# The two latent norms are emitted earlier in the projection stream of a hybrid FoX/MLA layer

## The chip, the cores and the metric

The kernel runs on one core of a Trainium2 chip. The metric is the device time of one execution in microseconds (us), the median of three runs. TensorE (PE, with its weight loads PEld), VectorE (DVE), ScalarE (ACT) and GpSimd (POOL) each work through one list of instructions in a fixed order. Loads are issued from SyncE's queue (SP), in order as well, and a few stores from POOL's.

## The reference, cut to what matters

One layer for 512 prompt tokens and 64 sample tokens, 576 together. One projection makes the FoX queries, keys and values and the two MLA latents, and each latent gets an RMS norm before it is used:

```
z = rmsnorm(x, g_attn) @ w_in
q, k, v, f_lin, q_c, c_kv, k_r = split(z)      # 512 | 512 | 512 | 8 | 384 | 256 | 32
fox  = softmax(q k' + forget) v                # 8 heads x 64
q_full = rmsnorm(q_c, g_q) @ w_q_up            # query latent, 384
c_kv   = rmsnorm(c_kv, g_kv)                   # key latent, 256, also an output
mla  = softmax(q_lat c_kv' + q_rope k_r') ...  # 8 heads
x = x + [fox, mla] @ w_out
x = x + (silu(conv(gate)) * conv(value)) @ w_down
```

## The kernel before, in words

Activations lie with features on the partitions and the 576 tokens along a row. A projection tile of 128 features (`in_tile`) is a product of 48 matmuls: 8 input chunks, 3 passes each (weights and activations are split in a high and a low part), for two halves of 288 tokens. The halves go to two PSUM banks that `psg` hands out. After the start these are the two banks with the tag `g`. DVE evacuates each half (L449, L455, L458 for keys, queries, values of a head pair, L542 for a latent), and only then may PE write that bank again.

FoX has four head pairs, p = 0 to 3. `fox_gemm(p)` projects the pair's keys, then its queries, then its values. An optional function `between` is called after the keys and before the queries. Behind pair 1 come the five latent tiles, a = 0 and 1 for the key latent (`craw`), a = 2 to 4 for the query latent (`qcr`). `sq_sum` squares the tiles of a latent and adds them up on DVE, POOL and ACT. `latent_norm` then does this: `col_sums` (L229) sums the squares over the partitions with a matmul against ones, one for each half, each shown as two passes in the trace, into two `g` banks; L261 evacuates them; L250 and L251 on ACT and L255 to L257 on DVE make the reciprocal root; L549 on DVE scales each tile of the latent.

Attention of a head is made of scores (L516, L517, L358, or for MLA L702 to L704), a softmax on DVE, ACT and POOL, transposes (L374) and values (L389). Each pair also has a sample part (L523, L524, L427, L437, for MLA L721, L722). `A` holds the stacked operands of a head, two buffers, filled by SP's L476 to L512, for MLA by L476 to L478 and L695 to L698, after the head before the last has given its buffer back. `mla_caches` loads the old rotary keys (`kr_T`, L633) into the buffer `spt` that the sample part of pair 3 gives back behind L437; L637, L638 and L639 split them into `cf`, which the last matmul of the MLA sample scores, L722, reads.

The emission order comes from a planner: five streams of work are interleaved by written costs and due times (`yield`). The build then sets the order of each engine from data, buffers and that emission order. So a moved call can shift much that stands behind it. `POOL` also issues the store of the key latent, `o_lat`.

Of the kernel before, what the change touches and what calls it, by code (L numbers as in the profile page):

```python
# [30 lines left out]
C_GA, C_GF, C_GL, C_GQ, C_GKV = 0, 8, 16, 24, 27  # L31
# [40 lines left out]
def build(nc, tc, io):  # L72
# [5 lines left out]
    V, S, G, PE = nc.vector, nc.scalar, nc.gpsimd, nc.tensor  # L78
# [9 lines left out]
    def raw():  # L88

        if ffn[0]:  # L90
            rawn[0] += 1
            tag, bufs = FRAW[rawn[0] % len(FRAW)]
            return sb([P, 580], F32, tag, bufs)
        return sb([P, 580], F32, "raw", RAW)
# [25 lines left out]
    def pick(kind):  # L120

        n = cyc[kind] = cyc.get(kind, -1) + 1
        return ENG[kind][n % len(ENG[kind])]
# [10 lines left out]
    def tt(kind, dst, a, b, op):  # L134
        (V if pick(kind) == "v" else G).tensor_tensor(dst, a, b, op=op)  # L135
# [76 lines left out]
    def evac(op, dst, ps, r=slice(0, P)):  # L212
        for hf, (o, w) in enumerate(HA):
            op(dst[:, o:o + w], ps[hf][r, :w], slice(o, o + w))

    def square(eng, t):
        s = raw()[:, :T]
        if eng is S:
            S.activation(s, t, AF.Square)
        else:  # L220
            eng.tensor_tensor(s, t, t, op=ALU.mult)
        return s

    def col_sums(tiles, w=ones):

        ps = psg()
        for hf, (o, wd) in enumerate(HA):
            for n, t in enumerate(tiles):
                PE.matmul(ps[hf][:, :wd], lhsT=w, rhs=t[:, o:o + wd], start=(n == 0), stop=(n == len(tiles) - 1))  # L229
        return ps  # L230

    def sq_sum(tiles, sq="sq", add="acc"):
        acc = None
        for t in tiles:
            s = square({"a": S, "v": V, "g": G}[pick(sq)], t)
            if acc is None:
                acc = s
            else:
                tt(add, acc, acc, s, ALU.add)
        return acc  # L240
# [18 lines left out]
    def rstd(ps, n, out):  # L259
        v, y, a = (raw()[:, :T] for _ in range(3))  # L260
        evac(lambda d, p, c: V.tensor_scalar(d, p, 1.0 / n, EPS, op0=ALU.mult, op1=ALU.add), v, ps)  # L261
        rstd_of(v, y, a, out)
# [28 lines left out]
    def in_tile(u, M=P):  # L291
        hl = wload(io["w_in"][u], 1024)
        ps = psg()
        gemm(ps, M, hl, xhl, HA)
        return ps
# [150 lines left out]
    def fox_gemm(p, between=None):  # L446
        ps = k0 if p == 0 else in_tile(p)
        k = raw()
        evac(lambda d, p, c: V.tensor_tensor(d, p, R[:, c], op=ALU.mult), k, ps)  # L449
        G.dma_start(io["o_k"][p], k[:, :T])  # L450
        if between:
            between()
        ps = in_tile(4 + p)
        q = raw()
        evac(lambda d, p, c: V.scalar_tensor_tensor(d, p, FOX_SCALE, R[:, c], op0=ALU.mult, op1=ALU.mult), q, ps)  # L455
        ps = in_tile(8 + p)
        v = raw()
        evac(lambda d, p, c: V.tensor_tensor(d, p, R[:, c], op=ALU.mult), v, ps)  # L458
        G.dma_start(io["o_v"][p], v[:, :T])
        return q, k, v  # L460
# [76 lines left out]
    craw, qcr = [], []  # L537
# [7 lines left out]
    def latent_norm(t, n, col, acc):  # L545
        r = raw()[:, :T]
        rstd(col_sums([acc]), n, r)
        for a in range(n // P):
            V.scalar_tensor_tensor(t[a], t[a], par[:, col + a:col + a + 1], r, op0=ALU.mult, op1=ALU.mult)  # L549
# [7 lines left out]
    fx = {0: fox_gemm(0)}  # L557
# [186 lines left out]
    def s_gemm():  # L744
        for p in range(1, 4):
            if p >= 2:
                yield ("after", ("stack", 2 * (p - 2) + 1), 0)
            fx[p] = fox_gemm(p, gates if p == 1 else None)
            yield ("done", 23.1, ("up", p))
            if p == 1:  # L750
                for a in range(5):
                    latent(a)
                    if a == 2:
                        rope_key()
                    if a == 1:
                        acc_c = sq_sum(craw)
                    if a == 4:
                        acc_q = sq_sum(qcr)
                    yield ("done", 7.7, ("lat", a))
            if p == 2:  # L760
                latent_norm(craw, 256, C_GKV, acc_c)
                latent_norm(qcr, 384, C_GQ, acc_q)
                for a in range(2):
                    G.dma_start(io["o_lat"][a], craw[a])
        mla_keys()
        yield ("done", 0, ("keys", 0))
        for p in range(4):
            if p == 0:
                yield ("after", ("stack", 5), 0)
            else:  # L770
                yield ("after", ("stack", 6 + 2 * p - 1), 0)
            if p % 2 == 0:
                q_rope(p // 2)
                yield ("done", 2.2, ("rope", p))
            mla_up(p)
            yield ("done", 5, ("up", 4 + p))
# [201 lines left out]
    for hf, (o, w) in enumerate(HC):  # L978
# [24 lines left out]
        v, y, a, r3 = (raw()[:, :w] for _ in range(4))  # L1003
# [121 lines left out]
```

## Time and profile before

| what | value |
| --- | --- |
| median of 3 runs | 796.04 us (795.74 to 796.42) |
| profiled execution | 796.07 us, span 794.2 us |
| PE busy | 766.0 us (96%) |
| PEld busy | 738.3 us (93%) |
| DVE, ACT, POOL busy | 504.4 us (64%), 340.9 us (43%), 265.5 us (33%) |
| granted TensorE clock | 0.995 of full speed |
| chain that ended last | PE 82%, DVE 5%, ACT 4%, DMA 4% |

The span runs from the first to the last instruction of the profiled execution. 1.9 us of that execution's time lie outside it. PE is busy nearly throughout, so what counts is where PE waits: any us in which PE does nothing is a us of the time.

### The profile page before, as it was taken

How to read it: one execution, taken by the hardware profiler on the slowest of the kernel's cores; microseconds unless marked ns; L12 is line 12 of the kernel's file. 1: busy time of each engine (PE TensorE's matmuls, PEld its weight loads, DVE VectorE, ACT ScalarE, POOL GpSimd, SP SyncE). 2: the span in 40 equal slices, each digit the busy share in tenths (PEclk: the TensorE clock that was granted, in tenths of full speed). 3: DMA queues.
4: the chain of work that ended last, by engine and by line, in shares of the span. 5: the costliest groups of instructions: out<-in, count | busy, mean ns of one | idle time of the engine just before them, and what ended most of it. 6: DMA issues, size and time to landing. Idle time of an engine off the chain costs nothing.

```text
span 794.2 us, 14259 instructions
## 1 busy us (share of the span) xinstructions
PE 766.0 (96%) x5582; PEld 738.3 (93%) x5582; DVE 504.4 (64%) x940; ACT 340.9 (43%) x612; POOL 265.5 (33%) x392
## 2 busy tenths in 40 slices
PE   8899999998999999999999999999999999999994
PEld 7899899887878889999999999999999999999994
DVE  6966735978676764656866424776326667675455
ACT  7426622568567773223434223333213443433232
POOL 5234532444132320432432221443122343332135
PEclk9999999999999999999999999999999999999997
DMA  9475325264545631222222232222222222222313
GB/s 328 142 205 143 99 80 156 93 180 134 146 105 127 156 106 36 75 89 86 75 83 77 65 106 89 80 81 62 80 100 89 96 81 80 80 67 85 95 53 119
DMA packets 33811, 83.97 MB, mean 106 GB/s; under 512 B 6007, under 2 KB 9351, under 8 KB 33745
## 3 DMA queue, kind: packets, MB, share of 16 engines
q1 hardware_dynamic: 31520, 78.55, 33.1%
q0 software_dynamic: 1008, 3.19, 1.1%
q10 hardware_dynamic: 1216, 1.33, 0.5%
q8 instruction: 44, 0.72, 0.4%
q14 instruction: 23, 0.18, 0.1%
HBM read 64.12 MB, written 5.49 MB: 88 GB/s over the span
## 4 chain that ended last, share of the span: by engine, by line
PE 82%; DVE 5%; ACT 4%; DMA 4%; issue 2%; SPq 1%; POOL 1%; POOLq 0%; ACTq 0%; DVEq 0%
PE g L209 36%; PE s L209 19%; PE t L209 12%; PE g L437 3%; PE g L990 1%; DMA mix<-xT 1%; PE t L374 1%; PE s L721 1%; ACT p L325 1%; DVE B L381 1%; PE s L990 1%; ACT wh L194 1%; PE s L890 1%; PE t L990 1%; DVE wh L135 1%
## 5 line engine op out<-in xcount | busy, mean ns | idle before, releaser
L209 PE MATMUL g<-xs,wh 128*128 128x288 f32 x1680 | 239.4, 296 | 0.4 <-ACT wh L194 0.2
L209 PEld LDWEIGHTS g<-xs,wh 128*128 128x128 f32 x1680 | 227.7, 188 | 1.8 <-ACT wh L194 0.4
L194 ACT ACTIVATE wh<-wr 128x1024 fp32r<-128x1024 f32 (+4 forms) x106 | 99.7, 943 | 195.1 <-PE g L209 75.4
L135 POOL TENSOR_TENSOR wh<-wr,wh 128x1024 fp32r<-128x1024 f32 (+3 forms) x51 | 111.3, 2182 | 161.2 <-ACT wh L194 131.1
L209 PE MATMUL s<-xs,wh 128*128 128x288 f32 (+1 forms) x504 | 75.3, 295 | 2.6 <-DVE xs L266 2.6
L209 PEld LDWEIGHTS s<-xs,wh 128*128 128x128 f32 (+1 forms) x504 | 69.0, 186 | 3.3 <-ACT wh L194 2.0
L135 DVE TENSOR_TENSOR wh<-wr,wh 128x1024 fp32r<-128x1024 f32 (+5 forms) x55 | 60.9, 1111 | 14.0 <-ACT wh L194 13.8
L209 PE MATMUL t<-xs,wh 128*128 128x288 f32 (+1 forms) x348 | 52.4, 295 | 1.4 <-DVE wh L135 1.4
L209 PEld LDWEIGHTS t<-xs,wh 128*128 128x128 f32 (+1 forms) x348 | 47.7, 185 | 1.8 <-DVE wh L135 1.6
L909 POOL COPY KR<-raw 128x2 f32<-128x2 f32 x33 | 15.6, 474 | 92.4 <-DVE raw L907 92.4
L331 POOL TENSOR_SCALAR p<-p,small 128x128 f32<-128x128 f32 (+2 forms) x48 | 27.3, 570 | 49.2 <-DVE small L326 37.3
L913 DVE SCALAR_TENSOR_TENSOR raw<-raw,par 128x578 f32<-128x578 f32 x22 | 33.4, 1518 | 15.4 <-ACT raw L912 15.4
L939 ACT ACTIVATE raw<-raw 128x578 f32<-128x578 f32 x22 | 15.1, 688 | 58.2 <-DVE raw L914 58.1
L325 ACT ACTIVATE p<-s,small 128x128 f32<-128x128 f32 (+1 forms) x64 | 33.6, 526 | 8.3 <-DVE small L360 6.5
L381 DVE TENSOR_TENSOR B<-t,B 128x512 fp32r<-128x512 f32 (+1 forms) x64 | 29.8, 480 | 6.5 <-ACT B L128 6.3
L128 ACT ACTIVATE B<-t 128x512 fp32r<-128x512 f32 (+1 forms) x64 | 26.3, 435 | 15.9 <-PE t L374 15.2
L360 DVE TENSOR_REDUCE small<-s 128x1 f32<-128x128 f32 (+1 forms) x64 | 30.6, 479 | 2.8 <-PE s L358 1.2
L913 DVE SCALAR_TENSOR_TENSOR raw<-pq,par,raw 128x578 f32<-128x578 f32 x11 | 24.0, 2181 | 11.1 <-ACT raw L912 11.1
L209 PE MATMUL g<-sk,wh 128*128 128x288 f32 x186 | 30.6, 297 | 0.4 <-ACT wh L194 0.4
L209 PE MATMUL s<-sk,wh 128*128 128x288 f32 x192 | 30.8, 296 | 0.2 <-ACT wh L194 0.2
L209 PE MATMUL s<-sv,wh 128*128 128x288 f32 x192 | 30.6, 295 | 0.0
L209 PE MATMUL g<-sv,wh 128*128 128x288 f32 x186 | 29.8, 296 | 0.0
(377 smaller groups left out, 1571.7 us busy)
## 6 DMA issues: line engine op xcount, KB each, us to landing
wr<-w_up SPq DMA_DIRECT2D x44, 512.0 KB
wr<-w_dn SPq DMA_DIRECT2D x24, 384.0 KB
wr<-w_in SPq DMA_DIRECT2D x16, 512.0 KB
A<-pq SPq DMA_DIRECT2D x32, 256.0 KB
mix<-xT SPq DMA_DIRECT2D x16, 288.0 KB
wr<-w_out SPq DMA_DIRECT2D x8, 512.0 KB
A<-pq SPq DMA_DIRECT2D x24, 128.0 KB
sk<-k_c SPq DMA_DIRECT2D x4, 512.0 KB
```

The costliest lines, as they stand in the source:

```text
L128: S.activation(dst, src, AF.Copy)
L135: (V if pick(kind) == "v" else G).tensor_tensor(dst, a, b, op=op)
L194: S.activation(hl[:, 0, a:b], r[:, a:b], AF.Copy)
L209: PE.matmul(ps[hf][:M, :w], lhsT=hl[:, wi, kc * M:(kc + 1) * M], rhs=acts[kc][:, xi, o:o + w], start=(kc == 0 and pi == 0), stop=(kc == n ...
L325: S.activation(p, src, AF.Exp, bias=nm, accum_out=sm[:, 0:1])
L331: (G if e == "g" else V).tensor_scalar(p, p, sm[:, 1:2], 1.0, op0=ALU.mult, op1=ALU.mult)
L360: V.reduce_max(nm[:, 0:1], s[:, :W], axis=AX.X, negate=True)
L381: V.tensor_tensor(ptj[:, 1, off:], t[:, :w], f(ptj[:, 0, off:]), op=ALU.subtract)
L437: PE.matmul(out, lhsT=v[:, j, :], rhs=spt[:, j, :], start=(j == 0), stop=(j == 8))
L909: G.tensor_copy(cs[:, ch, 0:2], u[:, 512:514])
L913: V.scalar_tensor_tensor(t, u[:, 1:579], par[:, C_CW + 44 + ch:C_CW + 44 + ch + 1], t, op0=ALU.mult, op1=ALU.add)
L990: PE.matmul(ps[:, :w], lhsT=whl[m][:, wi, kc * P:(kc + 1) * P], rhs=g2[kc][:, xi, c], start=(kc == 0 and pi == 0), stop=(kc == n - 1 and p ...
```

## The change

The norm of the key latent and the store of it are emitted right behind the last latent tile, before pair 2 is projected. The norm of the query latent is emitted inside the projection of pair 2, between its keys and its queries. Before, both stood behind the whole projection of pair 2. Nothing is computed differently.

```
@@ s_gemm
-            fx[p] = fox_gemm(p, gates if p == 1 else None)
+            fx[p] = fox_gemm(p, (None, gates, lambda: latent_norm(qcr, 384, C_GQ, acc_q), None)[p])
...
                     if a == 4:
                         acc_q = sq_sum(qcr)
+                    if a == 4:
+                        latent_norm(craw, 256, C_GKV, acc_c)
+                        for b in range(2):
+                            G.dma_start(io["o_lat"][b], craw[b])
                     yield ("done", 7.7, ("lat", a))
-            if p == 2:
-                latent_norm(craw, 256, C_GKV, acc_c)
-                latent_norm(qcr, 384, C_GQ, acc_q)
-                for a in range(2):
-                    G.dma_start(io["o_lat"][a], craw[a])
```

**PE at the last latent tiles.** The rows are matmuls with output, inputs, shape and count, in PE's order; L209 is the projection, L229 the column sums. A minus marks rows of before, a plus those of now.

```order
-L209 MATMUL g<-xs,wh 128x288 x240
-L229 MATMUL g<-raw,ones 128x288
+L209 MATMUL g<-xs,wh 128x288 x96
+L229 MATMUL g<-raw,ones 128x288 x2
+L209 MATMUL g<-xs,wh 128x288 x48
+L229 MATMUL g<-raw,ones 128x288 x2
+L209 MATMUL g<-xs,wh 128x288 x194
```

Two latent tiles, the keys, queries and values of pair 2 were one run of 240 matmuls, and the four column sums stood one by one among the attention work behind it. Now the two sums of the key latent stand behind the last latent tile and the two of the query latent behind the keys of pair 2. Then the rest of pair 2 and the first half of pair 3 follow without a break, while pair 3's 144 matmuls stood behind the attention work before.

**DVE at the same place, before.** From the last latent tile (L542) through the keys of pair 2 (L449).

```order
L542 TENSOR_TENSOR mix<-g,R 128x288 x2
L135 TENSOR_TENSOR raw<-raw 128x576
L449 TENSOR_TENSOR raw<-g,R 128x288 x2
L490 COPY sk<-raw 128x64
L135 TENSOR_TENSOR wh<-wr,wh 128x1024
```

**DVE at the same place, now.**

```order
L542 TENSOR_TENSOR mix<-g,R 128x288 x2
L261 TENSOR_SCALAR raw<-g 128x288 x2
L135 TENSOR_TENSOR raw<-raw 128x576
L255 TENSOR_TENSOR raw<-raw 128x576
L256 SCALAR_TENSOR_TENSOR raw<-raw 128x576
L257 SCALAR_TENSOR_TENSOR raw<-raw 128x576
L449 TENSOR_TENSOR raw<-g,R 128x288
L549 SCALAR_TENSOR_TENSOR mix<-mix,par,raw 128x576 x2
L449 TENSOR_TENSOR raw<-g,R 128x288
L261 TENSOR_SCALAR raw<-g 128x288
L490 COPY sk<-raw 128x64
```

The norm of the key latent now stands around the two evacuations of pair 2's keys: four instructions ahead of the first L449 (the L135 in between, which adds the last squares of the query latent, was there before), and the two L549 between the first and the second.

**PE behind the last FoX sample part, before.** L209 is here the query up-projection, L669 the key and value up-projection of an MLA pair, L374 and L389 belong to FoX head 7.

```order
L209 MATMUL g<-xs,wh 128x288 x15
L374 MATMUL t<-ident,p_2413 128x128
L374 MATMUL t<-ident,p_2424 128x128
L374 MATMUL t<-ident,p_2435 128x128
L209 MATMUL g<-xs,wh 128x288
L389 MATMUL o<-B,v 128x512
L669 MATMUL g<-xs,wh 128x512 x6
L374 MATMUL t<-ident,p_2424 128x128
L374 MATMUL t<-ident,p_2435 128x128
L389 MATMUL o<-B,v 128x512
L722 MATMUL s<-cf,sl 128x384
```

**PE at the same place, now.**

```order
L209 MATMUL g<-xs,wh 128x288 x11
L374 MATMUL t<-ident,p_2413 128x128
L374 MATMUL t<-ident,p_2424 128x128
L374 MATMUL t<-ident,p_2435 128x128
L722 MATMUL s<-cf,sl 128x384
L389 MATMUL o<-B,v 128x512
L669 MATMUL g<-xs,wh 128x512 x12
```

L722, which reads `cf`, moved ahead of the first L389, six L669 and two L374.

**SP at the same place, before.** Loads from the stack of the second MLA head (the second L476) to `kr_T`.

```order
L476 DMA A<-pq 64x512
L695 DMA A<-KR 2x512
L696 DMA A<-KR 4x512
L478 DMA A<-pq 64x2x512 x2
L698 DMA A<-qr 32x512
L477 DMA A<-pq 64x1024 x2
L698 DMA A<-qr 32x512 x2
L185 DMA wr<-w_qu 128x384
L686 DMA sl<-qr 32x64 x2
L626 DMA sv<-c_tok 128x1024
L633 DMA spt<-kr_T 32x1024
```

**SP at the same place, now.**

```order
L476 DMA A<-pq 64x512
L478 DMA A<-pq 64x2x512 x2
L695 DMA A<-KR 2x512
L477 DMA A<-pq 64x1024 x2
L696 DMA A<-KR 4x512
L698 DMA A<-qr 32x512 x3
L185 DMA wr<-w_qu 128x384
L626 DMA sv<-c_tok 128x1024
L633 DMA spt<-kr_T 32x1024
```

The two small loads L686 moved ahead of this piece; the rest is the same set.

## Rows read from the trace of the kernel before

**Rows 1.** Windows: length, then busy us (count) of PE, PEld, DVE, ACT, POOL; clock, DMA.

```profile
116.00:134.70 18.70, 18.70 (x143) 18.70 (x142) 9.33 (x11) 4.61 (x7) 7.07 (x5) 1.00 0.39 108
134.70:146.00 11.30, 10.59 (x62) 7.82 (x60) 10.58 (x27) 7.23 (x18) 2.69 (x6) 1.00 0.65 173
165.40:190.00 24.60, 22.52 (x149) 18.32 (x148) 21.55 (x53) 17.79 (x48) 14.17 (x19) 1.00 0.56 159
```

**Rows 2.** Timeline of PE: start, length, instruction, shapes, count, idle time ahead and releaser.

```profile
134.71 0.65 PE L229 MATMUL g<-raw,ones 128*128 128x288 f32 x2
135.19 0.38 PE L340 MATMUL t<-ident,raw 128*128 128x128 f32 x2
...
144.08 0.30 PE L374 MATMUL t<-ident,p 128*128 128x128 f32 x1 [0.28 <-DVE B L381]
...
145.42 0.45 PE L516 MATMUL s<-A 128*128 128x384 f32 x1 [0.43 <-ACT p L325]
```

**Rows 3.** Timeline of DVE, 108 to 147 us.

```profile
115.83 0.46 DVE L542 TENSOR_TENSOR mix<-g,R 128x288 f32<-128x288 f32 x1 [2.74 <-PE g L209]
117.60 2.96 DVE L135 TENSOR_TENSOR raw<-raw 128x576 f32<-128x576 f32 x1 [1.32 <-POOL raw L221]
...
122.19 0.46 DVE L449 TENSOR_TENSOR raw<-g,R 128x288 f32<-128x288 f32 x1 [1.26 <-PE g L209]
...
134.91 0.46 DVE L458 TENSOR_TENSOR raw<-g,R 128x288 f32<-128x288 f32 x1 [1.83 <-PE g L209]
135.40 0.46 DVE L261 TENSOR_SCALAR raw<-g 128x288 f32<-128x288 f32 x1
...
140.26 0.76 DVE L255 TENSOR_TENSOR raw<-raw 128x576 f32<-128x576 f32 x1 [0.28 <-ACT raw L251]
...
146.32 1.53 DVE L549 SCALAR_TENSOR_TENSOR mix<-mix,par,raw 128x576 f32<-128x576 f32 x2
```

**Rows 4.** Timeline of POOL, the subtraction that splits a projection tile's weights.

```profile
117.53 2.42 POOL L135 TENSOR_TENSOR wh<-wr,wh 128x1024 fp32r<-128x1024 f32 x1
```

**Rows 5.** Timeline of PE, 165 to 230 us.

```profile
191.46 0.23 PE L358 MATMUL s<-bfc 128*128 128x128 bf16 x1
...
194.07 0.39 PE L389 MATMUL o<-B,v 128*128 128x512 f32 x1
...
200.63 0.59 PE L721 MATMUL s<-sk,ql 128*128 128x384 f32 x2
...
205.74 0.40 PE L389 MATMUL o<-B,v 128*128 128x512 f32 x1
...
209.87 0.41 PE L722 MATMUL s<-cf,sl 96*128 96x384 f32 x1 [1.89 <-ACT cf L639]
```

**Rows 6.** Timeline of SP's queue, 165 to 232 us: start of issue, time to issue.

```profile
186.08 1.81 SPq L698 DMA_DIRECT2D A<-qr  x3
...
191.67 0.54 SPq L476 DMA_DIRECT2D A<-pq  x1
192.26 0.64 SPq L695 DMA_DIRECT2D A<-KR  x1
...
194.14 1.38 SPq L478 DMA_DIRECT2D A<-pq  x2
...
196.43 1.45 SPq L477 DMA_DIRECT2D A<-pq  x2
...
202.33 0.53 SPq L626 DMA_DIRECT2D sv<-c_tok  x1
202.97 0.36 SPq L633 DMA_DIRECT2D spt<-kr_T  x1
```

**Rows 7.** Timeline of ACT, 190 to 215 us.

```profile
203.48 0.60 ACT L128 ACTIVATE B<-t 128x512 fp32r<-128x512 f32 x1 [2.13 <-PE t L374]
...
207.34 1.11 ACT L637 ACTIVATE cf<-spt 32x1088 fp32r<-32x1088 f32 x1 [2.53 <-DMA spt<-kr_T]
208.48 1.11 ACT L639 ACTIVATE cf<-spt 32x1088 fp32r<-32x1088 f32 x1
```

## Prediction, made before the changed kernel ran

> **What bounds the kernel now.** I first read the busy shares in the table above: PE works for 766.0 of 794.2 us, no other engine over 64%. So the question is how long PE stands still in the stretches that the change reorders, from the last latent tiles to the first MLA heads; a few heads further on PE's list is the same again.
>
> Second, the windows of these stretches [rows 1]. In the projection of pair 2 (116.0 to 134.7 us) PE and its weight loads are busy without a pause, and DVE for half the time. In the attention stretch that holds both norms (134.7 to 146.0) PE is idle for 11.30 - 10.59 = 0.71 us, while DVE is busy for 10.58 of the 11.30. In the next attention stretch, behind pair 3's projection, PE is idle for 24.60 - 22.52 = 2.08 us.
>
> Third, PE's own timeline for the waits themselves. The 0.71 us are two, 0.28 us behind DVE and 0.43 us behind ACT [rows 2]. The longest wait of the whole region is further on: 1.89 us ahead of L722 [rows 5], which waits for the split of the old rotary keys on ACT, and that for their load [rows 7].
>
> **The change part by part.** The same instructions run before and after. PE's four column sums cost the same at either place: two passes take 135.19 - 134.71 = 0.48 us [rows 2], four of them 1.9 us, moved and not removed. So every term is a wait of PE that goes, comes or grows.
>
> *What goes.* The column sums, the four L261 and the first set of L255 to L257 leave the stretch where DVE is nearly full. I take both waits there as gone: -0.71 us. At worst nothing goes, 0. At best more goes than the idle time shows; that is a rival below.
>
> *The first new seam, behind the last latent tile.* A column sum needs two `g` banks, and PE has just filled them. Its first half can start at once, since the first half's bank was evacuated during the second half. Its second half needs the bank of L542's second evacuation, 115.83 + 0.46 = 116.29 [rows 3]. PE is free for it earlier. Where v's projection ended, the next matmul started 0.20 us ahead of the evacuation, 134.71 against 134.91 [rows 2, 3], so here PE is free at 115.63, and behind the first half's sum at 116.11. For the step from DVE's end to PE's start I take 0.2 us, an estimate below the 0.28 us from the end of L639 to L722 (209.87 - 209.59) [rows 5, 7]. So the second sum starts at 116.49: a bubble of about 0.4 us. The next projection needs the bank that L261 empties (0.46 us) from 116.3, free at about 117.0, when PE has also ended the second sum. So +0.4 us, and pair 2's keys run from 116.97.
>
> *The second new seam, behind the keys of pair 2.* The keys take 122.19 - 115.83 = 6.36 us, the distance of the last evacuations of two tiles that follow each other [rows 3], and end at 123.33; the first sum takes PE to 123.81. The second one needs L449's second evacuation, and DVE is late for it. In DVE's new order, L135 adds the last squares of the query latent: it took 2.96 us, from 117.60 to 120.56, since POOL's subtraction of 2.42 us ran from 117.53 [rows 3, 4], against 0.76 us for L255 of the same size. Both stand at the same place now. Behind it come L255 to L257 at 0.76 us each, the first L449 with 0.46, two L549 with 1.53 and the second L449 with 0.46, together 4.73 us, which with the overlap of one instruction's start with the end of the one before (0.08 us in the two L549 at 0.805 us) is about 4.2. The second L449 ends at about 124.8, PE starts the sum at 125.0: +1.2 us. If DVE were in time, this seam too would cost 0.4 us; without the overlap 1.7 us. Together the seams cost 1.6 us, from 0.8 to 2.1.
>
> What is left of the query latent's norm behind the second seam is an L261, L255 to L257 and three L549, 0.46 + 2.28 + 2.3 = 5.0 us on DVE. It runs under the queries and values of pair 2, where DVE has been idle for half of the 18.70 us [rows 1], and costs nothing; without that cover the evacuation of the queries would hold up the second half of the values. The two stores of the key latent now stand on POOL ahead of the store of pair 2's keys and the next weight subtraction. POOL is busy for 7.07 of 18.70 us there [rows 1], so I cost them at nothing.
>
> *L722 and the old rotary keys.* The order moves L722 ahead of an L389, six L669 and two L374, which covered its wait. I lay the new order out on the old clock from head 7's last score tile (191.46). Six L669 that followed it (to 194.07) now stand ahead of it, so PE reaches L721 2.57 us earlier, at 198.06 in place of 200.63 [rows 5]. What PE runs from there to L722 is what it ran to the L389 at 205.74: it is at L722 at 203.2. The load L633 needs `spt`, free behind L437, which ends as L721 starts, and its turn on SP: from L476 at 191.67, issue times 0.54, 1.38, 0.64, 1.45, 0.63 (L696 like L695), 1.81 for L698, 0.53 for L185 as for L626, 0.53 [rows 6], and some 0.4 us of pauses: L633 at 199.6. It took 207.34 - 202.97 = 4.37 us from its issue to L637 [rows 6, 7], with the same 512 KB load ahead of it as now. So L637 starts at 204.0, L639 ends 2.25 us later, and L722 starts 0.28 us after that, at 206.5. That is a wait of 3.3 us where there were 1.89: +1.4. ACT now runs its copy of `B` (0.60 us) and the evacuations of the query tile behind L639, no longer ahead of L637 [rows 7], and the L389 behind L722 waits for that copy: about 0.4 us more, an estimate. Queued behind L722 on PE are L669 and head 7's values, and ACT waits in L637 with head 7's next copies behind it. So +1.8 us. At one end the wait vanishes, -1.89. At the other SP is as late behind L437 as before (202.97 - 200.63 = 2.34 us, so 200.4 for 199.6): +2.6.
>
> *The merged attention.* Pair 3's projection no longer lies between the two stretches. I take their other waits as unchanged in sum.
>
> Sum, against the profiled execution's 796.07 us (the median is 796.04, so nothing is corrected): 796.07 - 0.71 + 1.6 + 1.8 = 798.8 us.
>
> **The rivals.**
>
> *The stretch gives back more than its idle time.* If DVE and not PE sets the pace of the stretch from 134.7 to 146.0, then taking the norms off it shortens it by more than 0.71 us. For it: DVE was busy for 94%, of which four L261 at 0.46 us and one set of L255 to L257 at 0.76 us make 4.1 us [rows 1, 3]. Against it: PE's list ran on there with 0.71 us of idle time. As a bound, PE's weight loads were busy for 7.82 of 11.30 us [rows 1], so at most 3.48 us could be hidden waiting. That gives 796.07 - 3.48 + 1.6 + 1.8 = 796.0: not slower. It decides from 3.4 us of hidden wait on. The Trainium skill (Perfetto Trace Analysis, Identifying the Most-Contended Engine) holds matmul busy time to be a poor measure and weight-load busy time a good one. By it the sum would be this 796.0. The trace agrees in the projection, where both are full, and leaves it open in the stretch, whose matmuls are partly long for their weights.
>
> *L722 waits as long as before.* If `kr_T` lands 1.8 us earlier than I laid out, since other loads left SP earlier, the time is 796.07 - 0.71 + 1.6 = 797.0. Against it: the load cannot be issued before L437 ends, at 198.1, and that alone saves 1.5 us.
>
> *The merged attention waits more.* Between the two stretches PE had 19.4 us of projection in which ACT, DVE and POOL caught up with their softmax work. In the stretch behind it DVE is busy for 21.55 of 24.60 us all the same [rows 1]. If without the break the idle time of that stretch doubles, 2.08 us are added: 800.9. Against it: the stretch also loses the norms' DVE work. The Trainium skill (Perfetto Trace Analysis, Optimization Strategy) says that interleaving regimes with different busiest engines can help. By it, pulling the projection together ahead of the attention is a loss, this 800.9; the trace shows both regimes, 9.33 of 18.70 us of DVE against 21.55 of 24.60, but no run with them apart.
>
> **How the numbers follow.** The forecast gets 0.42, more hidden waiting 0.14, L722 as before 0.24, more waiting in the merged attention 0.20. The time is 798.8 us. The range goes from 795.2, below the first rival (its 796.0 with the seams at their low end of 0.8), to 801.0, just above the third, which is also where the forecast ends with its terms at their upper bounds (796.07 + 2.1 + 2.6 = 800.8). Slower by over 0.2% (1.6 us, about what a measurement of this kernel can tell from no change) means above 797.6: nearly all of the forecast and of the third rival, 0.59. Within 0.2% lie most of the second and half of the first, 0.29. Faster gets the other half and the case that several bounds fall on their low side, 0.12.
>
> **What would show it.** Right: two short idle times of PE around L229 behind the latent tiles, the second the longer, with the second L449 ending about 1 us after the keys' last matmul; no idle time of PE in front of L374 and L516 where the norms stood; L722 with a wait of over 3 us behind L639. Wrong: L722 with 2 us or less, or an attention stretch of pairs 2 and 3 whose idle time differs from 2 us by more than one. The prediction is wrong as a whole if PE's idle time between 108 and 232 us does not grow.

## The result and the profile after

The changed kernel takes 802.73 us (median of 3 runs, 802.67 to 804.63) against 796.04: a ratio of 1.0078, 95% interval 1.0054 to 1.0102. The direction was forecast, the size was not: 798.8 was the number and 801.0 the end of the range. The profiled execution took 804.63 us, its span is 802.8 us.

The page's first section splits this span. PE's list is the same 5582 matmuls. They were busy for 769.1 us where they were busy for 766.0, and the rest of the span grew from 794.2 - 766.0 = 28.2 to 802.8 - 769.1 = 33.7 us. Read so, 5.5 us are more standing still, and 3.1 us are the same work taking longer. This split is rough: a matmul counts as busy up to a modelled end, so that part of a late start can lie inside the busy time.

The timeline of the changed kernel shows where PE stands still (start, length, engine, line, operation, tiles, shape, count, and in brackets the idle time ahead and its releaser), with the rows of other engines that set it:

```profile
115.36 1.47 PE L229 MATMUL g<-raw,ones 128*128 128x288 f32 x4
...
124.82 0.75 PE L229 MATMUL g<-raw,ones 128*128 128x288 f32 x2 [1.07 <-DVE raw L449]
...
157.76 0.81 PE L523 MATMUL s<-sk,qb 128*128 128x384 f32 x2
...
169.26 2.99 POOL L135 TENSOR_TENSOR xs<-wr,sk 128x1024 fp32r<-128x1024 f32 x1
172.20 0.72 POOL L331 TENSOR_SCALAR p<-p,small 128x512 f32<-128x512 f32 x1
...
172.97 0.66 PE L374 MATMUL t<-ident,p 128*128 128x128 f32 x4 [1.90 <-DVE small L360]
...
174.32 1.59 PE L523 MATMUL s<-sk,qb 128*128 128x384 f32 x2
...
198.09 0.41 PE L374 MATMUL t<-ident,p 128*128 128x128 f32 x2 [1.35 <-DVE B L381]
...
204.43 0.37 SPq L633 DMA_DIRECT2D spt<-kr_T  x1
...
208.90 1.11 ACT L637 ACTIVATE cf<-spt 32x1088 fp32r<-32x1088 f32 x1 [5.35 <-DMA spt<-kr_T]
210.03 1.11 ACT L639 ACTIVATE cf<-spt 32x1088 fp32r<-32x1088 f32 x1
...
211.42 0.66 PE L722 MATMUL s<-cf,sl 96*128 96x384 f32 x1 [3.60 <-ACT cf L639]
...
227.06 0.44 PE L702 MATMUL s<-A 128*128 128x384 f32 x1 [2.01 <-DVE sp L409]
```

The two L229 are the seams: the first follows without a gap that the row would name, the second waits 1.07 us. The wait of 3.60 us at L722 stands where 1.89 us stood [rows 5]; L633, L637 and L639 are the load and the split behind it [rows 6, 7]. New are the waits of 1.90 and 1.35 us, and that of 2.01 us is longer. The one ahead of L374 names DVE, but the four transposes read `p`, and `p` came from POOL's L331, which ended 0.05 us before them; it stood behind a POOL split of 2.99 us. The third thing is L523: two matmuls of the same shape took 0.81 us at 157.76 and 1.59 at 174.32.

The windows of the changed kernel say why. Their columns are span, PE, PEld, DVE, ACT and POOL busy with counts, the granted clock as a share of 2.4 GHz, and the DMA share:

```profile
core 0: us, PE busy (x) PEld busy (x) DVE busy (x) ACT busy (x) POOL busy (x), PEclk, DMA share, GB/s
108.00:157.40 49.40, 48.27 (x355) 46.98 (x354) 29.75 (x44) 16.23 (x25) 11.71 (x10) 1.00 0.40 119
157.40:173.60 16.20, 13.22 (x85) 10.43 (x84) 14.84 (x40) 10.64 (x29) 10.05 (x13) 1.00 0.62 173
173.60:177.00 3.40, 3.40 (x11) 2.07 (x10) 1.81 (x4) 1.78 (x5) 2.04 (x4) 0.50 0.53 129
177.00:211.10 34.10, 29.10 (x207) 25.66 (x206) 22.46 (x56) 23.43 (x57) 10.73 (x18) 1.00 0.48 123
211.10:214.60 3.50, 3.18 (x8) 2.57 (x9) 2.47 (x7) 3.44 (x12) 1.21 (x2) 0.51 0.00 0
214.60:228.20 13.60, 11.59 (x76) 10.70 (x75) 9.53 (x25) 7.83 (x18) 4.50 (x6) 1.00 0.57 145
228.20:231.60 3.40, 3.40 (x13) 2.92 (x13) 3.16 (x11) 2.40 (x10) 1.98 (x3) 0.50 0.24 69
231.60:330.00 98.40, 92.20 (x650) 85.04 (x650) 59.45 (x153) 59.47 (x146) 20.95 (x36) 1.00 0.40 102
```

Three times the granted clock is at half, 1.2 GHz: from 173.6, from 211.1 and from 228.2 us, each at or right behind one of the waits of 1.90, 3.60 and 2.01 us. In them PE works for 3.40 + 3.18 + 3.40 = 10.0 us, of which up to half is lost; PE's busy time grew by 3.1. In the profiled execution of before the clock is full up to the last 8 us, in this region too. The fall in the last 8 us, in both kernels, stands behind PE's last matmul (784.3 us in before, 792.7 in the changed kernel) and costs nothing.

A check comes from two points between which both kernels run the same work, with equal counts on each engine: from the end of the last latent tile (115.63 us in before, 115.36 in the changed kernel) to L736, a product of a later MLA sample. The timelines have L736 of before and of the changed kernel, and the windows reach up to it:

```profile
306.76 0.71 PE L736 MATMUL g<-raw,wm 128*128 128x128 f32 x4 [0.52 <-DVE raw L732]
```

```profile
315.16 0.71 PE L736 MATMUL g<-raw,wm 128*128 128x128 f32 x4 [0.52 <-DVE raw L732]
```

```profile
115.63:306.76 191.13, 179.88 (x1227) 161.23 (x1225) 138.36 (x324) 118.42 (x288) 64.36 (x89) 1.00 0.48 126
```

```profile
115.36:315.16 199.80, 182.15 (x1227) 164.17 (x1225) 135.44 (x324) 119.39 (x288) 62.99 (x89) 0.97 0.46 121
```

The stretch is 8.7 us longer, as the whole span is 8.6. The three windows at half clock lie in it, 10.3 us: at most 5.1 us are the clock, and at least 3.5 are more waiting.

There is a second accounting, over all timed runs and not one. Each run lists its span and its mean granted clock. Span times clock is an estimate of the time that the run would need at full clock; the rest, span times (1 - clock), is what the clock costs at most. The last 8 us at half clock make up some 4 us of it, in which PE has no work, so only differences between kernels count. For before, 64 runs taken beside the experiments have a mean span of 795.4 us at a clock of 0.9927, which is 789.6 and 5.8. The three runs of the changed kernel have 801.5 us at 0.9880, which is 791.9 and 9.6. So of 6.1 us of mean span, by this estimate **2.3 are more waiting and 3.8 are the clock**. With three runs of the changed kernel, each of the two is uncertain by nearly 2 us.

### The profile page after: what moved, and what is told of

Same layout as the page of the kernel before. It is cut to its first block, busy times and chain, and to the rows that moved or that the text cites. A ratio compares the mean times of both kernels' runs of the same rounds, so it can differ in the third digit from the quotient of the medians.

```text
span 802.8 us, 14264 instructions
## 1 busy us (share of the span) xinstructions
PE 769.1 (96%) x5582; PEld 741.9 (92%) x5582; DVE 502.2 (63%) x940; ACT 341.9 (43%) x612; POOL 264.7 (33%) x392
## 4 chain that ended last, share of the span: by engine, by line
PE 81%; DVE 5%; ACT 4%; DMA 4%; issue 2%; SPq 2%; POOL 1%; POOLq 0%; DVEq 0%; ACTq 0%
PE g L209 35%; PE s L209 18%; PE t L209 12%; PE g L437 3%; PE t L374 1%; PE g L989 1%; DMA mix<-xT 1%; PE o L389 1%; PE s L721 1%; DMA A<-qr 1%; PE s L989 1%; ACT p L325 1%; PE s L889 1%; PE t L989 1%; DMA A<-pq 1%
## 5 line engine op out<-in xcount | busy, mean ns | idle before, releaser
L209 PE MATMUL g<-xs,wh 128*128 128x288 f32 x1680 | 239.1, 296 | 0.2 <-ACT wh L194 0.2
L209 PEld LDWEIGHTS g<-xs,wh 128*128 128x128 f32 x1680 | 227.5, 188 | 1.7 <-ACT wh L194 0.4
L135 POOL TENSOR_TENSOR wh<-wr,wh 128x1024 fp32r<-128x1024 f32 (+3 forms) x51 | 111.8, 2192 | 171.4 <-ACT wh L194 147.5
L209 PE MATMUL s<-xs,wh 128*128 128x288 f32 (+1 forms) x504 | 75.3, 295 | 1.6 <-DVE xs L266 1.6
L209 PEld LDWEIGHTS s<-xs,wh 128*128 128x128 f32 (+1 forms) x504 | 69.0, 185 | 2.3 <-ACT wh L194 1.5
L135 DVE TENSOR_TENSOR wh<-wr,wh 128x1024 fp32r<-128x1024 f32 (+5 forms) x55 | 60.8, 1111 | 13.8 <-ACT wh L194 13.6
L209 PE MATMUL t<-xs,wh 128*128 128x288 f32 (+1 forms) x348 | 52.4, 295 | 1.3 <-DVE wh L135 1.3
L209 PEld LDWEIGHTS t<-xs,wh 128*128 128x128 f32 (+1 forms) x348 | 47.7, 185 | 1.7 <-DVE wh L135 1.6
L331 POOL TENSOR_SCALAR p<-p,small 128x128 f32<-128x128 f32 (+2 forms) x48 | 26.1, 546 | 52.0 <-DVE small L326 43.4
L374 PE MATMUL t<-ident,p 128*128 128x128 f32 x160 | 29.2, 276 | 4.3 <-DVE small L360 1.9
L209 PE MATMUL g<-sk,wh 128*128 128x288 f32 x186 | 30.6, 297 | 0.4 <-ACT wh L194 0.4
L209 PE MATMUL s<-sk,wh 128*128 128x288 f32 x192 | 30.8, 295 | 0.1
L209 PE MATMUL s<-sv,wh 128*128 128x288 f32 x192 | 30.6, 295 | 0.0
```

The source lines that it names most:

```text
L209: PE.matmul(ps[hf][:M, :w], lhsT=hl[:, wi, kc * M:(kc + 1) * M], rhs=acts[kc][:, xi, o:o + w], start=(kc == 0 and pi == 0), stop=(kc == n ...
L331: (G if e == "g" else V).tensor_scalar(p, p, sm[:, 1:2], 1.0, op0=ALU.mult, op1=ALU.mult)
L374: PE.transpose(t[:, P * (i - j):P * (i - j + 1)], st["p"][i][:, P * j:P * (j + 1)], ident)
```

## The experiments

At first I held two theories. **A**: pair 3's projection has moved ahead of the attention, whose softmax work and loads lost their cover. **B**: the column sums between projection tiles are the cost. The first four runs left neither as it stood, and **C** came out of them: waits of PE cost their length and, through the clock, something again. The table has medians, ratios with their intervals, and the accounting above (means over the runs). Each ratio goes against the runs of before on the same chip, whose median moved between 796.2 and 797.6 us from one chip to the next; the row of before has the runs on four chips together.

| kernel | runs | median us | ratio to before | clock | span x clock | lost to clock |
|---|---|---|---|---|---|---|
| before | 64 | 797.1 | | 0.9927 | 789.6 | 5.8 |
| changed | 3 | 802.7 | 1.0054 to 1.0102 | 0.9880 | 791.9 | 9.6 |
| key_only | 6 | 804.0 | 1.0053 to 1.0107 | 0.9870 | 791.6 | 10.4 |
| query_only | 7 | 802.2 | 1.0036 to 1.0093 | 0.9867 | 790.4 | 10.6 |
| hold3_both | 11 | 802.3 | 1.0049 to 1.0090 | 0.9865 | 790.2 | 10.8 |
| late_norms | 5 | 809.0 | 1.0108 to 1.0167 | 0.9822 | 792.6 | 14.4 |
| after_krwr | 6 | 801.5 | 1.0039 to 1.0082 | 0.9870 | 789.4 | 10.4 |
| before_krwr | 10 | 793.8 | 0.9937 to 0.9977 | 0.9936 | 787.1 | 5.1 |
| before_kr2x | 12 | 798.2 | 0.9989 to 1.0023 | 0.9931 | 790.5 | 5.5 |
| after_fill | 6 | 801.6 | 1.0047 to 1.0110 | 0.9885 | 791.9 | 9.2 |
| fill3 | 6 | 802.3 | 1.0051 to 1.0089 | 0.9928 | 794.4 | 5.7 |
| ct_dve | 6 | 804.6 | 1.0077 to 1.0131 | 0.9872 | 792.5 | 10.3 |
| krwr_ct | 10 | 799.9 | 1.0019 to 1.0049 | 0.9903 | 789.9 | 7.7 |
| fill_proj | 6 | 808.4 | 1.0120 to 1.0184 | 0.9863 | 796.3 | 11.0 |

### Halves of the change

**key_only** moves the key latent's norm alone, with its two stores.

```
+                    if a == 4:
+                        latent_norm(craw, 256, C_GKV, acc_c)
+                        for b in range(2):
+                            G.dma_start(io["o_lat"][b], craw[b])
...
             if p == 2:
-                latent_norm(craw, 256, C_GKV, acc_c)
                 latent_norm(qcr, 384, C_GQ, acc_q)
-                for a in range(2):
-                    G.dma_start(io["o_lat"][a], craw[a])
```

> Only the key latent's norm and its two stores are moved; the query latent's norm stays behind pair 2's projection. PE's order: the seam behind the last latent tile is there, the one inside pair 2 is not, the first third of pair 3's projection (48 matmuls) moves ahead of head 2's and 3's scores, and its other 96 stand a little earlier than before. Theory A (pair 3's projection moved ahead of the attention, which lost its cover): the attention still has two thirds of the projection between its pieces, so at most a third to a half of the loss shows: 796 to 799 us, with no wait of over 2.5 us ahead of L722. Theory B (the column sums between projection tiles are the cost): the first seam was 0.07 us of idle time, the second 1.07, so without the second nearly all the loss is gone: 796.0 to 796.5 us, whatever the attention does.

**query_only** moves the query latent's norm alone.

```
-            fx[p] = fox_gemm(p, gates if p == 1 else None)
+            fx[p] = fox_gemm(p, (None, gates, lambda: latent_norm(qcr, 384, C_GQ, acc_q), None)[p])
...
             if p == 2:
                 latent_norm(craw, 256, C_GKV, acc_c)
-                latent_norm(qcr, 384, C_GQ, acc_q)
```

> Only the query latent's norm is moved, into pair 2's projection; the key latent's norm stays behind it. PE's order: the second seam is there, the first third of pair 3's projection moves ahead of the scores as in the other half of the change, its second third stands between head 2's score tiles. Theory A: as the other half alone, 796 to 799 us; the sum of the two halves' losses is well under the whole change's 6.7 us, since only both together bring pair 3's projection ahead. Theory B: nearly the whole loss is here, 801 to 802.5 us, with the idle time of PE around the second pair of L229.

Each half costs as much as the whole, 804.0 and 802.2 us. A's 796 to 799 is missed by both, and B's 796.0 to 796.5 by key_only. B's figure for query_only came out, but not for B's reason: that execution has no wait of over 1 us at its seam. PE stood still for 0.06 us in all between 108 and 160 us. So the seam's 1.07 us in the changed kernel needs the key latent's norm ahead of it on DVE, as the prediction worked it out. What each half has instead is a long wait in the attention, and the clock at half there. The timelines show PE's longest waits of key_only and of query_only, one row each:

```profile
178.07 0.80 PE L437 MATMUL g<-spt,sv 128*128 128x128 f32 x2 [4.37 <-DVE spt L431]
```

```profile
183.71 0.79 PE L516 MATMUL s<-A 128*128 128x512 f32 x1 [2.68 <-ACT p L325]
```

The granted clock is 0.50 from 177.7 to 187.8 us in the one and from 183.6 to 190.4 in the other.

### Pair 3's projection held back, or moved ahead alone

**hold3_both** is the changed kernel with pair 3's projection emitted later and ordered behind a score tile.

```
-                yield ("after", ("stack", 2 * (p - 2) + 1), 0)
+                yield ("after", ("s", 3) if p == 3 else ("stack", 1), 0)
...
+            if p == 3:
+                with tc.issue_after(last["s"]):
+                    fx[p] = fox_gemm(p)
...
```

> The whole change, and pair 3's projection emitted only once head 3's first score tile is emitted, and ordered on PE behind the score tile emitted last. Both seams stay as they are in the changed kernel; the 144 matmuls of pair 3 lie between the attention's pieces again, more finely than before. Theory A: the waits of 1.90, 1.35 and the growth at L722 go or shrink below 1 us, the granted clock is full up to the kernel's last stretch, and the time falls to 794 to 798 us. Theory B: the seams stay, so 801 to 803 us.

**late_norms** is the kernel before with both norms behind pair 3's projection.

```
-            if p == 2:
+            if p == 3:
                 latent_norm(craw, 256, C_GKV, acc_c)
                 latent_norm(qcr, 384, C_GQ, acc_q)
```

> The opposite half: both norms are emitted behind pair 3's projection, where they stood behind pair 2's. No column sum lies between projection tiles, and pair 3's projection runs straight behind pair 2's, as it does in the changed kernel; the norms' work on DVE falls into the merged attention. Theory A: the attention has lost its cover as in the changed kernel, and has the norms on DVE besides: 800 to 806 us, with waits of PE over 1 us in the merged attention and a fall of the granted clock behind one of them. Theory B: no seams, so 795.5 to 797 us.

B falls here: late_norms has no seam and is the slowest of these at 809.0 us. (For hold3_both B's 801 to 803 us came out, but its seam waits the same 1.07 us, and its longer waits lie further on.) A is half right. Moving the projection ahead without the seams is worse than the change, as A says, and worse than its 806, with the norms' DVE work in the attention as well; giving the cover back does not bring the time back, 802.3 us. The timeline of hold3_both has the wait at L374 gone (its lines are up to two higher, L724 is L722), but not those further on:

```profile
190.91 3.00 PE L671 MATMUL g<-xs,wh 128*128 128x512 f32 x12 [1.51 <-DVE mix L394]
...
214.84 0.66 PE L724 MATMUL s<-cf,sl 96*128 96x384 f32 x1 [3.68 <-DVE cf L640]
...
228.20 0.50 PE L390 MATMUL o<-B,v 128*128 128x512 f32 x1 [1.85 <-ACT B L128]
```

In late_norms the waits lie in the merged attention:

```profile
167.56 0.70 PE L389 MATMUL o<-B,v 128*128 128x512 f32 x1 [2.34 <-ACT B L128]
...
177.12 0.39 PE L389 MATMUL o<-B,v 128*128 128x256 f32 x1 [2.48 <-DVE B L381]
...
219.95 0.58 PE L389 MATMUL o<-B,v 128*128 128x256 f32 x1 [3.17 <-ACT B L128]
```

and its windows at just these places:

```profile
167.70:174.50 6.80, 6.50 (x20) 4.36 (x20) 6.80 (x14) 3.77 (x13) 3.26 (x5) 0.50 0.50 119
177.90:184.70 6.80, 5.73 (x25) 5.32 (x24) 4.21 (x8) 2.98 (x5) 2.64 (x2) 0.50 0.42 136
218.90:225.70 6.80, 5.75 (x18) 5.18 (x19) 5.89 (x14) 4.71 (x14) 1.82 (x3) 0.50 0.35 121
```

Span times clock rose by 0.6 to 3.0 us in the four, the loss to the clock by 4.6 to 8.6. Against the 17 runs of before on their own chip (790.1 and 5.3 us) it is the same picture: by 0.0 to 2.5 and by 5.1 to 9.0. From here on theory C is on trial.

### One wait taken away

**after_krwr** loads `kr_T` into a tile of the weight ring. It was a tile of `spt`, which a FoX sample held. **before_krwr** does the same in the kernel before.

```
-        krc = sb([32, 1152], F32, "spt", 1)
-        nc.sync.dma_start(krc[:, :PAST], io["kr_T"])
-        V.tensor_copy(krc[:, PAST:KEYS], gate["krs"])
+        krc = sb([P, 1024], F32, "wr", 2)[:32]
+        nc.sync.dma_start(krc, io["kr_T"])
...
+        for src, o, w in ((krc, 0, PAST), (gate["krs"], PAST, NS)):
+            S.activation(KS[0:32, o:o + w], src, AF.Copy)
...
```

> The changed kernel, with the load of kr_T into a tile of the weight ring, so that it waits neither for the spt tile nor behind the MLA heads' stacks on SP; its split into cf waits for the last FoX sample score alone. Theory C (each long wait of PE costs its own length and then again, since the granted clock falls to 1.2 GHz behind it): the wait of 3.6 us ahead of L722 goes, and with it the 3.41 us at half clock at 211; the time falls by 3 to 5 us, to 798 to 800 us, and the mean clock rises from 0.988 to 0.990 or more. Theory A' (the waits alone, the clock is a bystander): 3 us at most, to 800 us, with the clock as low as before. Rival D (the wait moves to another consumer of the same late work, such as head 7's values): no gain, 802 to 803 us.

> The same edit in the kernel before, where L722 waited 1.89 us and the clock did not fall in the profiled execution (in 17 others the mean clock lay between 0.989 and 0.995 and the time between 794.4 and 800.9 us). Theory C: the wait goes and with it the executions at the lower clock become fewer: 793 to 796 us. Theory A': 794 to 795 us. Rival D: 796 us.

The wait at L722 is gone in both; the timeline of before_krwr has the row without a bracket:

```profile
203.50 0.34 PE L722 MATMUL s<-cf,sl 96*128 96x384 f32 x1
```

Span times clock falls by 2.5 us in both (791.9 to 789.4, 789.6 to 787.1), so the load was the cause of this wait, and the prediction's step on it holds. But in the changed kernel the clock stays low: it no longer falls at 211 us, it falls at 193.3, behind another wait, and the time drops by 1.2 us where C expected 3 to 5. The 21 runs of before on the same chip had 789.4 us of span times clock too, and 6.5 lost to the clock where after_krwr loses 10.4: what is left of the loss there is the clock. In the kernel before the whole gain arrives. **before_krwr beats both kernels**: 793.8 us, ratio 0.9957, interval 0.9937 to 0.9977. The timeline of after_krwr with the waits that stayed or came:

```profile
173.05 1.11 PE L374 MATMUL t<-ident,p 128*128 128x128 f32 x4 [1.89 <-DVE small L360]
...
191.70 0.39 PE L389 MATMUL g<-B,v 128*128 128x256 f32 x1 [1.64 <-ACT B L128]
```

**before_kr2x** was to add a wait: `kr_T` loaded twice.

```
+        nc.sync.dma_start(krc[:, :PAST], io["kr_T"])
```

> The kernel before, with kr_T loaded twice into the same tile, so that the second load waits for the first and L722 waits some 2 to 3 us longer (4 to 5 us); nothing is computed differently, and PE's order differs in a dozen rows only. Theory C: the clock falls to 1.2 GHz at or behind that wait for 3.4 to 6.8 us, and the time rises by the added wait and 1.7 to 3.4 us more: 799.5 to 802 us, mean clock 0.990 or less. Theory A': the added wait alone, 798 to 799 us, mean clock 0.993 as before.

It told nothing. PE's order moved other work ahead of L722 (L723 there), whose wait was 1.09 us and not longer, and the time is that of before. The 798 to 799 us of A' came out, but without the added wait that they were to stand for.

**ct_dve** takes the 2.99 us split off POOL, **krwr_ct** joins it to after_krwr.

```
-"cTl": "gggv"
+"cTl": "vvvv"
```

> The changed kernel with the two low splits of c_T (128x1024) on DVE in place of POOL, where one of 2.99 us stood ahead of the scaling of head 4's last tile. Theory C with theory A: the wait of 1.90 us at 171 shrinks below 1 us, and the clock does not fall at 173; the other two falls stay: 800 to 801.5 us, mean clock 0.990. Rival F (DVE is as full as POOL in this stretch, so that the wait moves to DVE's next consumer): a wait of 1 to 2 us elsewhere between 165 and 195 us with its own fall, 802 to 804 us.

> The changed kernel with both edits: kr_T through the weight ring, and c_T's low splits on DVE. Theory C: both long waits with their falls are gone, the time is what the edits give one by one, 801.5 less 2 us: 798.5 to 800 us, mean clock 0.991 or more; still behind the kernel before with the kr_T edit alone (793.8), by the seam of 1.07 us and the waits that have no cover. Rival F: 801 to 803 us.

ct_dve went as its rival F had it: a wait of 1.63 us behind DVE at the same place, with a fall of the clock at 176.7 us, and 804.6 us, just above F's 802 to 804. With the `kr_T` edit as well the time is 799.9, the best of the kernels with both norms moved, and the clock 0.9903, just under what C expected. That time lies in C's range by luck: C had both long waits and their falls gone, but the profiled execution has waits of 1.71 and 1.64 us and the clock at half for 3.4 us behind each, from 177.1 and 197.6 us.

### Waits filled with useless work

These runs test C directly. **after_fill** puts 14 useless matmuls behind L721, where PE then waits for `kr_T`.

```
...
+            if d["first"] and c == 0:
+                w_ = bank("o")
+                for n in range(14):
+                    PE.matmul(w_, lhsT=ql[:, 0, 0:P], rhs=ml["T"][0][0][:, :512], start=True, stop=True)
```

> The changed kernel, with 14 matmuls of 512 columns behind L721, into a bank that nothing reads: some 3.2 us of work of PE in the time in which it waits ahead of L722, ordered a few rows ahead of L722. PE's idle time ahead of L722 falls from 3.6 us to about 0.5; L722 itself starts no earlier, since the load sets its start. Theory C: the clock no longer falls at 211, and the time falls by about 1.7 us, to 800.5 to 801.5 us, with useless work added. Theory A': the same wait for the same load, 802.7 us or more, and the clock falls where it fell, or the fillers make it later by what they overrun.

**fill3** has these 14 and fills two waits more, with column-sum matmuls of 288 columns.

```
+FILL = {(4, 0, 3): 4}
...
+                if (st["h"], j, i) in FILL:
+                    w_ = bank("o")
+                    for n in range(FILL[st["h"], j, i]):
+                        PE.matmul(w_[:, :288], lhsT=ones, rhs=par[:, :288], start=True, stop=True)
...
+            if st.get("fill") and g == 1:
+                for _ in range(3):
+                    PE.matmul(t[:, :288], lhsT=ones, rhs=sp[:, :288], start=True, stop=True)
```

> The changed kernel with useless matmuls in three of PE's waits, into banks that nothing reads from them: 14 of 512 columns ahead of L722 as in the run before, 4 column-sum matmuls of 288 columns (about 1.9 us) in the wait of 1.90 us ahead of head 4's transposes, and 3 of them (about 1.4 us) beside the wait of 1.35 us at 198. PE works some 6.5 us more and waits some 6.5 us less. Theory C (the falls of the granted clock follow from PE's waits, and make up some 4 us of the 6.7): no fall at 171, 198 and 211 us, mean clock 0.993 or more, and the time falls by 3 to 5 us to 797.5 to 800 us although useless work is added. Rival E (the falls come from something else in this stretch, such as the work of the other engines): the falls stay, mean clock 0.988, 801 to 804 us.

**fill_proj** is the control: about the same amount of useless work at the seam inside pair 2's projection.

```
+        if p == 2:
+            w_ = bank("o")
+            for n in range(14):
+                PE.matmul(w_[:, :288], lhsT=ones, rhs=k[:, :288], start=True, stop=True)
```

> The control for the run with useless matmuls in three waits: the changed kernel with about as much useless work of PE (14 column-sum matmuls of 288 columns, some 6.6 us) at the seam inside pair 2's projection, where PE hardly waits; PE's order behind it is that of the changed kernel, and its waits from 165 us on should stay. Theory C (filling the waits is what kept the clock up): the clock falls behind the waits as in the changed kernel, mean clock 0.986 to 0.989, and the time rises by the added work less the seam's 1.07 us, to 807 to 809.5 us. Rival G (more work of PE, wherever it stands, keeps the clock up): mean clock 0.992 or more, 803 to 805 us.

In after_fill the clock no longer fell at 211 or 228 us; it fell at 171 for 6.8 us and at 198 for 3.4, at the waits that were not filled. The time is 801.6 us, at the upper end of what C expected but hardly for its reason: as much time lies at half clock as in the changed kernel, and the loss to it is 9.2 us against 9.6. In fill3 the clock fell nowhere in the region. Two of its fillers in the timeline (L378 in the wait of 1.90 us, L733 ahead of L722, which is L734 there and waits no more), and the window of the whole region:

```profile
174.65 2.21 PE L378 MATMUL o<-par,ones 128*128 128x288 f32 x8 [0.31 <-DVE mix L398]
...
211.25 3.46 PE L733 MATMUL o<-sk,ql 128*128 128x512 f32 x14
...
215.98 0.36 PE L734 MATMUL s<-cf,sl 96*128 96x384 f32 x1
```

```profile
165.00:235.00 70.00, 63.26 (x397) 53.09 (x396) 49.69 (x132) 48.34 (x127) 29.64 (x42) 1.00 0.54 141
```

PE still stands still for 6.7 of these 70 us, but in no piece of over 1.15 us. The clock over its six runs is 0.9928, that of before, and the loss to it 5.7 us; ct_dve, on the same chip and with its waits unfilled, had 0.9872 and 10.3. In the control the waits stayed, and the clock fell behind each, as the timeline (L726 is L722, L706 is L702) and the windows show:

```profile
178.41 0.66 PE L374 MATMUL t<-ident,p 128*128 128x128 f32 x4 [1.89 <-DVE small L360]
...
216.23 0.41 PE L726 MATMUL s<-cf,sl 96*128 96x384 f32 x1 [2.35 <-ACT cf L643]
...
232.94 0.44 PE L706 MATMUL s<-A 128*128 128x384 f32 x1 [2.66 <-DVE sp L409]
```

```profile
179.70:183.10 3.40, 3.40 (x13) 2.69 (x12) 1.52 (x4) 1.37 (x5) 1.38 (x4) 0.50 0.69 145
...
217.20:220.60 3.40, 3.40 (x9) 2.66 (x9) 2.63 (x8) 2.82 (x10) 1.01 (x1) 0.51 0.23 67
...
234.30:237.70 3.40, 3.40 (x14) 3.02 (x13) 2.98 (x11) 2.21 (x10) 1.98 (x3) 0.50 0.00 0
```

About the same useless work brings the mean clock from 0.9880 to 0.9928 in the waits and to 0.9863 outside them. So the falls follow from PE's waits: that is C against E and G. (The control's work stands some 50 us ahead of the first of these waits; useless work close by but outside them was not tried.) The mean span is 801.5 us for the changed kernel, 800.2 for fill3 and 807.4 for the control. The 5.8 us of the control are clear of the scatter, the 1.4 of fill3 are not, and waits that are filled would leave the time as it was without any effect of the clock. In the time fill3 missed its 797.5 to 800 us: by the accounting the clock gave back 3.9 us, and the fillers overran the waits by 2.5 (span times clock 791.9 to 794.4). So that the falls follow the waits is shown; that they cost some 4 us of time rests on the accounting and the windows, not on a time that came back.

## Why the prediction was off

The step that failed is the sentence "So every term is a wait of PE that goes, comes or grows". PE's own work took longer too, at half clock: some 3.8 us of the 6.1 over all runs, at most 5.1 of the 8.7 in the profiled execution. No term of the sum stood for it. The waits alone came near the 2.8 us of the sum: 2.3 over all runs, 3.5 or a little more in the profiled execution.

**The waits that go, -0.71 us: right.** Between the second seam and the attention PE stood still for nothing, and no wait stands where the norms stood.

**The seams, +0.4 and +1.2: right.** The idle time shows 0.07 and 1.07 us, but part of a late start lies inside the busy time. At the first seam the next projection started 1.30 us behind the first column sum, where the two sums alone take 0.96 (twice the 0.48 of [rows 2]): some 0.3. The second sum started at 116.08, 0.05 us behind L542's second evacuation, as was worked out. At the second seam the projection started 2.19 us behind the first sum: some 1.2, and that wait stands behind the L449 that was named. Together about 1.6, the 1.6 of the sum. Rows of PE's timeline in the changed kernel, then one from a window at the second sum, then DVE's:

```profile
116.66 6.59 PE L209 MATMUL g<-xs,wh 128*128 128x288 f32 x48
123.08 0.66 PE L229 MATMUL g<-raw,ones 128*128 128x288 f32 x2
...
125.27 26.01 PE L209 MATMUL g<-xs,wh 128*128 128x288 f32 x194
```

```profile
116.08 0.51 PE L229 MATMUL g<-raw,ones 128*128 128x288 f32 x1
```

```profile
115.57 0.46 DVE L542 TENSOR_TENSOR mix<-g,R 128x288 f32<-128x288 f32 x1 [2.74 <-PE g L209]
...
124.31 0.45 DVE L449 TENSOR_TENSOR raw<-g,R 128x288 f32<-128x288 f32 x1
```

**L722, +1.8: right.** The wait is 3.60 us against 1.89, +1.71. It was worked out as +1.4 here and +0.4 at the L389 behind it, where no idle time shows; that the sum fits so closely is in part luck. after_krwr shows that it is the load.

**The merged attention, "I take their other waits as unchanged in sum": too low.** From the seams' end to L721, without the stretch's own two waits of 0.28 and 0.43 us, PE stood still for 3.5 us before and stands still for 4.7 now, +1.2. Further on L702 waits 2.01 us for 0.77, and in the MLA heads behind it (256 to 282 us in before, 263 to 290 now) L702 2.17 for 0.92 and L704 1.20 for 0.30, which the sum put at nothing. The idle time overstates this: of the 3.5 us of waiting up to L736, the terms above (-0.71, 1.6 and 1.71) leave about 1 us for all of it. The third rival had the mechanism, the cover that is lost, and 800.9 us. Its place shows in the L331 behind which PE waited 1.90 us. In the timeline of before POOL scaled the same tile long before it was needed, while pair 3's projection ran:

```profile
148.72 0.91 POOL L331 TENSOR_SCALAR p<-p,small 128x512 f32<-128x512 f32 x1
```

Its reader, the transposes of head 4, followed 20 us later. Now L331 ends at 172.92 with POOL's long split ahead of it, and PE is there first. The Trainium skill (Perfetto Trace Analysis, Optimization Strategy) says that interleaving regimes may help. late_norms, with the projection in one piece, agrees by 3.0 us of span times clock, though it has the norms' work in the attention besides. hold3_both agrees by 1.7 us against the change, which is within the scatter of the three runs.

**The clock: missing altogether, the step that failed.** 3.8 of the 6.1 us are the granted clock by the accounting, and no term, rival or bound priced it. The profile of before gave a warning that was easy to pass over: the wait of 1.89 us was there without a fall, so I took waits to cost their length. The Trainium skill (TensorE: Matmul & The Clock Gate, Terms) puts the penalty at throttled time times the share of pulses withheld; by it the 10.3 us of the three windows at half clock cost 5.1, an estimate. The trace agrees in kind: PE worked for 10.0 us in them, and L523 took 1.59 us there for 0.81 outside. PE's busy time grew by 3.1 only, but it also holds waiting and so cannot decide the size.

**The first rival, hidden waiting given back, 796.0: wrong in the time.** It rested on weight-load time as the measure (the Trainium skill, Perfetto Trace Analysis, Identifying the Most-Contended Engine). Span times clock rose in the change and fell in none of the variants with a norm moved alone, so nothing came back in the time. Some hidden waiting may have gone all the same: up to L736 the same matmuls kept PE busy for 182.15 us, of which up to 5.1 are the clock, against 179.88 before, so at full clock for up to 2.8 us less, while the idle time rose by 6.4. No run separates the two. The second rival, L722 as before, fell with the 3.60.

**What stays open.** Which waits the clock falls behind is not settled: one of 1.34 us in after_fill had a fall, the 1.89 of before and a 2.17 of the changed kernel (at 263 us) had none. A wait could not be added to the kernel before to see it fall there, since its order closed around it.

## What to carry to other kernels

A kernel that keeps PE 96% busy has little to gain from a better place for some 10 us of VectorE work and much to lose from a stretch in which PE waits in pieces of 1.5 to 4 us: each may be paid once as a wait and again at half clock behind it. Read span and granted clock together, run by run: over several runs their product tells waiting from clock. A single run does not: over 64 runs of one kernel the product scatters nearly as much as the span (1.6 and 1.7 us). And when work is moved, look for what stood between them: here a projection that covered other engines' work slid ahead, and moving the load that was late anyway (`kr_T`) made the kernel before 0.4% faster, where the change made it 0.8% slower.

## What was unexpected in the hardware

The granted clock is not the same from run to run of one kernel: before had 0.989 to 0.997 over 64 runs, with 794.1 to 801.3 us. Part of that lies where no edit reaches: in the profiled executions of query_only, fill3, ct_dve and krwr_ct the clock was at half for 6.8 us from about 23 us on, in that of before_kr2x for 3.4 us from 8 us on, and in the others, before among them, at neither place.
